# The output projection of a hybrid attention and pooling block by one level of Strassen's scheme

## Chip, core, metric

The kernel runs on one core of a Trainium2 chip. The metric is the device time of one execution in microseconds (us); lower is better. Engines: TensorE (PE: matmuls, and PEld: its weight loads), VectorE (DVE), ScalarE (ACT), GpSimd (POOL) and SyncE (SP), which here issues all DMAs. Each engine runs its own list of instructions in order and waits for the others by semaphores.

## The reference

One layer over 4096 tokens of width 1024, all in float32, cut to what matters:

```python
mod = c @ w_ada[l] + b_ada[l]
shift, scale, gate = jnp.split(mod, 3, axis=-1)
h = rms_norm(x, norm_g[l]) * (1.0 + scale[:, None, :]) + shift[:, None, :]
proj = h @ w_in[l]                       # q, k, v, u, z
...
a_out = chunk_attention(q, k, v, rel_bias[l])
p_out = multiscale_pool(u, w_pool[l], pool_scale[l])
y = jnp.concatenate([a_out, p_out], axis=-1) * jax.nn.silu(z)
x = x + gate[:, None, :] * (y @ w_out[l])
```

The change concerns the last line: y (4096 x 1024) times w_out (1024 x 1024), times a gate of each column, plus x.

## The kernel before

Tokens are cut into 32 blocks of 128, the contraction into 8 k-tiles of 128, the output columns into two halves of 512. For precision every float32 operand of a matmul is split into a high part `hi` (a cast to fp32r by ScalarE) and a rest `lo` (a subtraction of it, by GpSimd or VectorE): that is `split`, L95 to L97, which issues one instruction on each of the two engines. A product of two tiles then takes three matmuls: hi·hi, hi·lo and lo·hi.

The stages follow one another in the program, and a scheduler orders each engine's instructions by a simulated timeline. Stage A makes h, z, u and the pooled half of y. Stage B is the attention: 64 units (2 phases x 8 groups of tokens x 4 heads); `merge` weaves the parts of two units and the filler `work` of the unit together by position. Units 0 to 57 have the q, k, v projections as filler. Units 58 to 63 have the output projection of 12 blocks (`plan[58 + n // 2]`), of the first column half alone, since `y` of these blocks is complete by then. y lies transposed in DRAM (`yT_d`). Stage C, the last `with` of the program (L758 on), is the rest: 4 blocks of half 0, 16 blocks of both halves, 16 blocks of half 1. Its pools take memory that the attention's pools free at the end of unit 63; the gate's tiles (L760 to L762) are among them.

`out_items` (L412 to L443) is a block's work. For each column half it takes a PSUM tile `ps` (pool `pp`, two banks) and issues 8 x 3 matmuls (L428 to L430, each 128x512); while it runs, `load_h` (L102) loads and splits the next block's y (ScalarE and GpSimd). At the end VectorE multiplies `ps` by the gate (L435), x is added (L437: by GpSimd in the units, by VectorE in stage C), and the result is stored (L438). In all 32 x 2 x 24 = 1536 matmuls.

What comes at the swap of stages B and C: `load_wo(1, 2)` and `load_wo(1, 3)` for the last weights, `fin` of the last attention unit (L663, L664, L666 with `osum`), then `out_items` without other work.

## Time and profile before

| what | us |
|---|---|
| median of three runs (1988.44 to 1990.84) | 1988.89 |
| the profiled execution | 1987.33 |
| its span in the trace | 1985.0 |
| TensorE busy in it | 1932.2 (97%) |
| VectorE, ScalarE, GpSimd busy | 1139.5, 892.0, 852.1 |

The profiled execution is one execution, recorded by the hardware; between its span and its time lie 2.3 us that the trace does not cover. Matmuls overlap in the array, so a record's duration (392 ns) is longer than the distance of two matmuls. Line numbers are those of the kernel before; those of the changed kernel, where they are named, differ.

### The profile page before, as it was taken

The page shows a single profiled execution, that of the slowest core. Times are in us where ns is not written, and L with a number is a line of the kernel's source. Part 1 is how long each engine was busy: PE and PEld are TensorE (multiplying, and loading weights), DVE is VectorE, ACT ScalarE, POOL GpSimd, SP SyncE. Part 2 cuts the span into 40 slices and gives each one's busy share as a digit, 9 for nine tenths or more (in the row PEclk, how much of TensorE's full clock was granted, in tenths as well). Part 3 has the DMA queues.
Part 4 walks back from the last instruction along what each step waited for, and adds up shares of the span by engine and source line. Part 5 has one row for each costly group of instructions (what it writes and reads, how often), then busy time and mean ns, then how long its engine had stood idle before and what let it go on. Part 6 is the DMA issues. An engine that isn't in the chain of part 4 may idle for free.

```text
span 1985.0 us, 30104 instructions
## 1 busy us (share of the span) xinstructions
PE 1932.2 (97%) x10544; PEld 1659.5 (84%) x10544; DVE 1139.5 (57%) x2331; ACT 892.0 (45%) x1910; POOL 852.1 (43%) x1423
## 2 busy tenths in 40 slices
PE   6989999999999999999999999999999999999999
PEld 5778888888888898888889888888888788788887
DVE  7656554565644557666776666667666654433322
ACT  5422123221224556655676665656666754311121
POOL 6232332133046654454465556444364644322243
PEclk9999999999999999999999999999999999999999
DMA  9555344435432212221132222111121444544454
GB/s 329 195 175 161 93 146 138 149 108 154 142 122 65 68 51 59 56 62 47 55 91 86 62 78 75 50 53 54 53 65 44 139 138 134 159 142 147 147 181 164
DMA packets 172231, 220.15 MB, mean 111 GB/s; under 512 B 17456, under 2 KB 93744, under 8 KB 172080
## 3 DMA queue, kind: packets, MB, share of 16 engines
q1 hardware_dynamic: 172080, 218.23, 34.9%
q8 instruction: 83, 1.36, 0.3%
q14 instruction: 68, 0.56, 0.1%
HBM read 151.05 MB, written 58.74 MB: 106 GB/s over the span
## 4 chain that ended last, share of the span: by engine, by line
PE 88%; DVE 5%; DMA 3%; ACT 2%; issue 1%; POOL 1%; SPq 0%; DVEq 0%; POOLq 0%; ACTq 0%
PE ps L494 9%; PE ps L495 9%; PE ps L496 9%; PE ps L430 6%; PE ps L429 6%; PE ps L428 6%; PE ptps L622 6%; PE aps L297 4%; PE aps L298 4%; PE aps L296 4%; PE ps L297 4%; PE ps L298 4%; PE ps L296 4%; PE sps L582 3%; PE ops L641 3%; PE ops L640 3%
## 5 line engine op out<-in xcount | busy, mean ns | idle before, releaser
L97 POOL TENSOR_TENSOR bhl<-bhr,bhh 128x512 fp32r<-128x512 f32 x212 | 275.7, 1301 | 334.8 <-ACT bhh L96 322.4
L494 PE MATMUL ps<-w,bhh 128*128 128x512 f32 (+1 forms) x1024 | 354.3, 346 | 2.7 <-ACT qkr L507 2.5
L496 PE MATMUL ps<-w,bhl 128*128 128x512 f32 (+1 forms) x1024 | 351.5, 343 | 0.0
L495 PE MATMUL ps<-w,bhh 128*128 128x512 f32 (+1 forms) x1024 | 351.5, 343 | 0.0
L629 DVE TENSOR_TENSOR ptl<-ptps,pth 128x512 fp32r<-128x512 f32 x480 | 226.0, 486 | 167.8 <-ACT pth L628 163.8
L96 ACT CAST bhh<-bhr 128x512 fp32r<-128x512 f32 x224 | 138.7, 620 | 283.6 <-PE ps L429 177.7
L600 ACT ACTIVATE p<-p,mx 128x640 f32<-128x640 f32 (+4 forms) x256 | 204.6, 799 | 125.6 <-DVE mx L587 123.7
L628 ACT CAST pth<-ptps 128x512 fp32r<-128x512 f32 x480 | 193.8, 425 | 136.9 <-PE ptps L622 111.2
L587 DVE CUSTOM_DVE_ANT_0 p<-sps,nb 128x640 f32<-128x640 f32 (+4 forms) x256 | 198.8, 777 | 81.1 <-PE sps L583 78.1
L622 PE MATMUL ptps<-ident,p 128*128 128x128 f32 x1200 | 213.0, 274 | 0.3
L494 PEld LDWEIGHTS ps<-w,bhh 128*128 128x128 f32 x1024 | 193.5, 189 | 21.7 <-ACT qkr L507 3.6
L496 PEld LDWEIGHTS ps<-w,bhl 128*128 128x128 f32 x1024 | 193.6, 189 | 17.8
L495 PEld LDWEIGHTS ps<-w,bhh 128*128 128x128 f32 x1024 | 193.7, 189 | 17.5
L428 PE MATMUL ps<-w,bhh 128*128 128x512 f32 x512 | 200.8, 392 | 2.5 <-DVE qkr L435 2.1
L430 PE MATMUL ps<-w,bhl 128*128 128x512 f32 x512 | 200.7, 392 | 0.1
L429 PE MATMUL ps<-w,bhh 128*128 128x512 f32 x512 | 200.5, 392 | 0.0
L259 POOL TENSOR_TENSOR xt<-xt,rb 128x512 f32<-128x512 f32 x56 | 80.0, 1462 | 234.0 <-DMA rb<-rs_d 234.0
L640 PE MATMUL ops<-pth,v 128*128 128x512 f32 x480 | 162.7, 340 | 4.1 <-ACT pth L628 2.6
L582 PE MATMUL sps<-kr,qs 128*128 128x320 f32 (+2 forms) x480 | 156.3, 334 | 7.6 <-DVE mx L587 6.8
L622 PEld LDWEIGHTS ptps<-ident,p 128*128 128x128 f32 x1200 | 147.2, 140 | 19.7 <-DVE ql L547 0.7
L641 PE MATMUL ops<-ptl,v 128*128 128x512 f32 x480 | 155.2, 330 | 1.8 <-DVE ptl L629 1.3
L297 PE MATMUL aps<-hlo,w 128*128 128x512 f32 x392 | 154.2, 393 | 2.1 <-DVE hlo L97 2.1
(129 smaller groups left out, 3885.6 us busy)
## 6 DMA issues: line engine op xcount, KB each, us to landing
bhr<-hT_d SPq DMA_DIRECT2D x128, 256.0 KB, 2.8
bhr<-yT_d SPq DMA_DIRECT2D x96, 256.0 KB, 2.9
xt<-in_x_dram SPq DMA_DIRECT2D x32, 512.0 KB, 5.1
qkr<-in_x_dram SPq DMA_DIRECT2D x64, 256.0 KB, 3.4
out_dram<-qkr SPq DMA_DIRECT2D x64, 256.0 KB, 2.2
xt<-in_xT_dram SPq DMA_DIRECT2D x28, 512.0 KB, 6.2
hT_d<-xt SPq DMA_DIRECT2D x56, 256.0 KB, 2.3
w_s<-in_w_adaT_dram SPq DMA_DIRECT2D x16, 512.0 KB, 6.7
```

The costliest lines, as they stand in the source:

```text
L97: eng.tensor_tensor(lo, raw, hi.bitcast(F32), op=ALU.subtract)
L297: nc.tensor.matmul(ps, wh[:, cs], l_, start=False, stop=False)
L428: nc.tensor.matmul(ps, a_, wh, start=k == 0, stop=False)
L429: nc.tensor.matmul(ps, a_, wl, start=False, stop=False)
L430: nc.tensor.matmul(ps, l_, wh, start=False, stop=k == KT - 1)
L494: nc.tensor.matmul(ps, a_, wh, start=k == 0, stop=False)
L495: nc.tensor.matmul(ps, a_, wl, start=False, stop=False)
L496: nc.tensor.matmul(ps, l_, wh, start=False, stop=k == KT - 1)
L582: nc.tensor.matmul(o, QS[ph, sg, h][:, qc], ks[:, k0 : k0 + n], start=True, stop=False)
L622: nc.tensor.transpose(out=ps[:, i * P : (i + 1) * P], in_=Pt[ph, sg, h, i][:, w : w + P], identity=ident)
L629: nc.vector.tensor_tensor(l_[:, r], ps[:, r], a_[:, r].bitcast(F32), op=ALU.subtract)
L640: nc.tensor.matmul(o[:, r], v, a_[:, r], start=n == 0, stop=False, skip_group_check=True)
```

## The change

One level of Strassen's scheme (in Winograd's form, with fewer additions) for pairs of blocks p and p + 16: the two blocks of tokens, the two halves of the contraction and the two halves of the columns make a 2 x 2 problem, and seven products of quarters, of 12 matmuls each, take the place of eight. That is 84 matmuls a pair.

Two of the seven need no combination. They are the *osteps* (32 of them, each 4 k-tiles x 3 matmuls): `(0, p)` multiplies the first half of y of block p by the first quarter of the weights, and ScalarE copies the result (L470) to be stored in DRAM (`s1_d`); `(1, p)` adds the second half's product in the same PSUM bank and finishes the first column half of block p (L473 gate on VectorE, L474 x on GpSimd). Both use the `ps` tiles and `load`-ahead by two. 24 osteps are planned in the units 58 to 63, where 12 half blocks were, with as many matmuls (288); eight come behind.

Then stage C. `w_prep`, four times, loads four weight tiles of 128x512, makes three more from them (L811 and L813 on VectorE, L812 and L816 on GpSimd) and splits four (three on VectorE, one on GpSimd). The *steps* follow, five products per pair in the order (1,p), (3,p), (2,p+1), (4,p), (0,p), each 12 matmuls (L420 to L422). For a pair, `combine` makes four combinations of y's quarters on GpSimd (L841 to L844) and five splits (ScalarE, and VectorE L98); five additions out of PSUM (L864, L867, L868, L871, L874), three gate multiplies (L426) on VectorE and three additions of x on GpSimd (L427) end it. Each pair has 11 DMAs of 256 KB. The pools: `d_w` of 16 weight tiles (4 before), `dr` of 12 raw tiles, `dc` of 3, and two PSUM pools (`dy`, `dz`) of two banks each.

```diff
@@ -409,38 +410,72 @@
-    def out_items(key, b, ns, after=None):
...
+    def product(ps, a_, l_, W, start):
+        for k in range(4):
+            wh, wl = W[k]
+            nc.tensor.matmul(ps, a_[:, k, :], wh, start=start and k == 0, stop=False, skip_group_check=True)
+            nc.tensor.matmul(ps, a_[:, k, :], wl, start=False, stop=False, skip_group_check=True)
+            nc.tensor.matmul(ps, l_[:, k, :], wh, start=False, stop=k == 3, skip_group_check=True)
+
+    def finish(c, n, xr, b, eng):
+
+        nc.vector.tensor_tensor(c, c, gate[n], op=ALU.mult)
+        eng.tensor_tensor(c, c, xr, op=ALU.add)
+        nc.sync.dma_start(out[b * P : (b + 1) * P, n * 512 : (n + 1) * 512], c)
...
+    osteps = [(0, 0)]
+    for p in range(1, NPAIR):
+        osteps += [(0, p), (1, p - 1)]
+    osteps.append((1, NPAIR - 1))
...
+            raw = sh.tile([P, 4, P], F32, name="bhr", bufs=2)
+            sg, j = divmod(p, NB)
+            nc.sync.dma_start(raw, yT_d[sg][j, :, half * 4 : half * 4 + 4, :])
+            a_ = sh.tile([P, 4, P], F32R, name="bhh")
+            l_ = sh.tile([P, 4, P], F32R, name="bhl")
+            split(a_, l_, raw, nc.gpsimd)
...
+            wh, wl = WO[0, half * 4 + k]
+            nc.tensor.matmul(ps, a_[:, k, :], wh, start=half == 0 and k == 0, stop=False, skip_group_check=True)
+            nc.tensor.matmul(ps, a_[:, k, :], wl, start=False, stop=False, skip_group_check=True)
+            nc.tensor.matmul(ps, l_[:, k, :], wh, start=False, stop=k == 3, skip_group_check=True)
+            if k == 3:
+                OH.pop(i)
+                o_load(i + 2)
+                t = op.tile([P, 512], F32, name="qkr")
+                if half == 0:
+                    nc.scalar.copy(t, ps)
+                    nc.sync.dma_start(s1_d[p], t)
+                else:
+                    nc.vector.tensor_tensor(t, ps, gate[0], op=ALU.mult)
+                    nc.gpsimd.tensor_tensor(t, t, xr, op=ALU.add)
+                    nc.sync.dma_start(out[p * P : (p + 1) * P, 0:512], t)
...
-        for n, ko in enumerate(outs):
-            plan[58 + n // 2].append(ko)
+        for i in range(24):
+            plan[58 + i // 4].append(("o", i))
...
-        w3 = cd.enter_context(tc.tile_pool(name="d_w", bufs=4))
+        w3 = cd.enter_context(tc.tile_pool(name="d_w", bufs=16))
...
+        dr = cd.enter_context(tc.tile_pool(name="d_r", bufs=12))
+        dc = cd.enter_context(tc.tile_pool(name="d_c", bufs=3))
+        dy = cd.enter_context(tc.tile_pool(name="d_y", bufs=2, space=PSUM))
+        dz = cd.enter_context(tc.tile_pool(name="d_z", bufs=2, space=PSUM))
...
-        rest = [("r", b, [0]) for b in range(NOUT, NOUT + 4)]
-        rest += [("r", b, [0, 1]) for b in range(NOUT + 4, NBLK)] + [("s", b, [1]) for b in range(NOUT + 4)]
...
+        def w_prep(k):
+            r = {}
+            for i in range(2):
+                for n in range(2):
+                    r[i, n] = dr.tile([P, 512], F32, name="dr")
+                    nc.sync.dma_start(r[i, n], wo[:, 4 * i + k, n * 512 : n * 512 + 512])
+            nc.vector.tensor_tensor(r[0, 0], r[0, 1], r[0, 0], op=ALU.subtract)
+            nc.gpsimd.tensor_tensor(r[0, 1], r[1, 1], r[0, 1], op=ALU.subtract)
+            nc.vector.tensor_tensor(r[1, 1], r[1, 1], r[0, 0], op=ALU.subtract)
+            w_split(2, k, r[1, 1], nc.vector)
+            w_split(1, k, r[0, 0], nc.vector)
+            nc.gpsimd.tensor_tensor(r[1, 0], r[1, 0], r[1, 1], op=ALU.subtract)
+            w_split(3, k, r[0, 1], nc.vector)
+            w_split(4, k, r[1, 0], nc.gpsimd)
+        WT[0] = {k: WO[1, 4 + k] for k in range(4)}
...
+        steps = [(2, 0)]
+        for p in range(NPAIR):
+            steps += [(1, p), (3, p)] + ([(2, p + 1)] if p + 1 < NPAIR else []) + [(4, p), (0, p)]
...
+            g = nc.gpsimd
+            if t == 2:
+                s1 = RAW[p, 2, 0] = dr.tile([P, 4, P], F32, name="dr")
+                g.tensor_tensor(s1, RAW[p, 1, 0], RAW[p, 1, 1], op=ALU.add)
+                g.tensor_tensor(RAW[p, 1, 0], RAW[p, 0, 0], RAW[p, 1, 0], op=ALU.subtract)
+                g.tensor_tensor(RAW[p, 0, 0], s1, RAW[p, 0, 0], op=ALU.subtract)
+                g.tensor_tensor(RAW[p, 0, 1], RAW[p, 0, 1], RAW[p, 0, 0], op=ALU.subtract)
+            raw = {2: RAW[p, 0, 0], 1: RAW.get((p, 2, 0)), 3: RAW[p, 1, 0], 4: RAW[p, 1, 1], 0: RAW[p, 0, 1]}[t]
+            a_ = sh.tile([P, 4, P], F32R, name="bhh")
+            l_ = sh.tile([P, 4, P], F32R, name="bhl")
+            split(a_, l_, raw, nc.vector)
...
+            last = nc.vector if p == NPAIR - 1 else nc.gpsimd
+            a_, l_ = DH.pop((t, p))
+            product(ps, a_, l_, WT[t], t in (1, 2))
+            if t == 2:
+                U2[p] = dc.tile([P, 512], F32, name="u2")
+                nc.vector.tensor_tensor(U2[p], ps, SX[p], op=ALU.add)
+            elif t == 3:
+                c = op.tile([P, 512], F32, name="qkr")
+                nc.vector.tensor_tensor(c, ps, SX[p], op=ALU.add)
+                nc.vector.tensor_tensor(c, ZP[p], c, op=ALU.add)
+                finish(c, 1, xr, b2, nc.gpsimd)
+            elif t == 4:
+                nc.vector.tensor_tensor(SX[p], ps, SX[p], op=ALU.add)
+                finish(SX.pop(p), 0, xr, b2, nc.gpsimd)
+            elif t == 0:
+                nc.vector.tensor_tensor(U2[p], ps, U2[p], op=ALU.add)
+                finish(U2.pop(p), 1, xr, p, last)
+
+        for i in range(24, len(osteps)):
+            if i < 28:
+                w_prep(i - 24)
+            for f in o_items(i):
                 f()
-            if i in (1, 2):
-                load_wo(1, i + 1, w3, stage)
+            if i == 28:
+                fetch(0)
+        combine(*steps[0])
+        combine(*steps[1])
+        for i, (t, p) in enumerate(steps):
+            if t == 1 and p + 1 < NPAIR:
+                fetch(p + 1)
+            step(t, p)
+            if i + 2 < len(steps):
+                combine(*steps[i + 2])
```

**The swap, on GpSimd.** In the list before, this stands around the end of the last attention unit (`osum` is the attention's last result; `w` and `bhl` are lower parts of weights and of y):

```order
L97 TENSOR_TENSOR bhl<-bhr,bhh 128x512 x3
L606 COPY rlx<-rl 128x4x64
L666 TENSOR_TENSOR osum<-osum,gzb 128x512
L606 COPY rlx<-rl 128x4x64
L97 TENSOR_TENSOR w<-bhr,w 128x512 x2
L97 TENSOR_TENSOR bhl<-bhr,bhh 128x512 x2
L97 TENSOR_TENSOR w<-bhr,w 128x512 x2
L97 TENSOR_TENSOR bhl<-bhr,bhh 128x512 x2
L666 TENSOR_TENSOR osum<-osum,gzb 128x512
L97 TENSOR_TENSOR bhl<-bhr,bhh 128x512 x62
```

and this in the list after, from the same `osum` (the `dr` are weights or y's quarters, in combination; `qkr` are finished blocks):

```order
L701 TENSOR_TENSOR osum<-osum,gzb 128x512
L474 TENSOR_TENSOR qkr<-qkr 128x512
L812 TENSOR_TENSOR dr<-dr 128x512
L816 TENSOR_TENSOR dr<-dr 128x512
L812 TENSOR_TENSOR dr<-dr 128x512
L474 TENSOR_TENSOR qkr<-qkr 128x512
L98 TENSOR_TENSOR bhl<-bhr,bhh 128x512
L816 TENSOR_TENSOR dr<-dr 128x512
L98 TENSOR_TENSOR w<-dr,w 128x512
L812 TENSOR_TENSOR dr<-dr 128x512
L98 TENSOR_TENSOR bhl<-bhr,bhh 128x512
L98 TENSOR_TENSOR w<-dr,w 128x512
```

Behind `osum` came splits of y only, each with its own block; now the first 24 instructions behind it, up to the first L843, are a mixture of the weights' combinations and splits, osteps' splits and ends, and the first combinations of y.

**The swap, on TensorE.** L640 and L641 (L675 and L676 after) are the attention's last products, L622 (L657) its transposes; `ps` are the output projection. Before:

```order
L429 MATMUL ps<-w,bhh 128x512
L430 MATMUL ps<-w,bhl 128x512
L640 MATMUL ops<-pth,v 128x128
L641 MATMUL ops<-ptl,v 128x128
L428 MATMUL ps<-w,bhh 128x512
L429 MATMUL ps<-w,bhh 128x512
L640 MATMUL ops<-pth,v 128x256
L641 MATMUL ops<-ptl,v 128x256
L640 MATMUL ops<-pth,v 128x128
L641 MATMUL ops<-ptl,v 128x128
L430 MATMUL ps<-w,bhl 128x512
L428 MATMUL ps<-w,bhh 128x512
```

After, the same place:

```order
L675 MATMUL ops<-pth,v 128x384
L676 MATMUL ops<-ptl,v 128x384
L657 MATMUL ptps<-ident,p 128x128 x2
L675 MATMUL ops<-pth,v 128x128
L657 MATMUL ptps<-ident,p 128x128
L676 MATMUL ops<-ptl,v 128x128
L675 MATMUL ops<-pth,v 128x256
L676 MATMUL ops<-ptl,v 128x256
L675 MATMUL ops<-pth,v 128x128
L676 MATMUL ops<-ptl,v 128x128
L462 MATMUL ps<-w,bhh 128x512
L463 MATMUL ps<-w,bhh 128x512
```

The output matmuls stood among the attention's last ones; now they follow them. Behind row L462 there are 72 osteps' matmuls (six osteps), then the steps.

**The loop over pairs, on VectorE.** Before, the last stage of the projection had these two in turn to the end:

```order
L437 TENSOR_TENSOR qkr<-qkr 128x512
L435 TENSOR_TENSOR qkr<-ps,gate_19468 128x512
L437 TENSOR_TENSOR qkr<-qkr 128x512
L435 TENSOR_TENSOR qkr<-ps,gate_19468 128x512
L437 TENSOR_TENSOR qkr<-qkr 128x512
```

After, from one pair of blocks to the next (`s_`, `u_` and `qkr` hold sums, `zps` and `yps` are PSUM):

```order
L867 TENSOR_TENSOR qkr<-yps,s_19971 128x512
L98 TENSOR_TENSOR bhl<-dr,bhh 128x512
L868 TENSOR_TENSOR qkr<-zps,qkr 128x512
L426 TENSOR_TENSOR qkr<-qkr,gate_19534 128x512
L864 TENSOR_TENSOR u_20151<-yps,s_20090 128x512
L98 TENSOR_TENSOR bhl<-dr,bhh 128x512
L871 TENSOR_TENSOR s_19971<-yps,s_19971 128x512
L98 TENSOR_TENSOR bhl<-dr,bhh 128x512
L426 TENSOR_TENSOR s_19971<-s_19971,gate_19532 128x512
L874 TENSOR_TENSOR u_20032<-zps,u_20032 128x512
L98 TENSOR_TENSOR bhl<-dr,bhh 128x512
L426 TENSOR_TENSOR u_20032<-u_20032,gate_19534 128x512
```

With one more split that makes 13 instructions a pair, five of them out of PSUM. 

**The loop over pairs, on GpSimd.** Before there were only L97 splits of `bhl` (the last row of the first list). After:

```order
L427 TENSOR_TENSOR s_19754<-s_19754,qkr 128x512
L842 TENSOR_TENSOR dr<-dr 128x512
L427 TENSOR_TENSOR u_19838<-u_19838,qkr 128x512
L843 TENSOR_TENSOR dr<-dr 128x512
L844 TENSOR_TENSOR dr<-dr 128x512
L427 TENSOR_TENSOR qkr<-qkr 128x512
L841 TENSOR_TENSOR dr<-dr 128x512
L427 TENSOR_TENSOR s_19852<-s_19852,qkr 128x512
```

That is seven a pair, four combinations and three ends.

## Rows read from the trace of the kernel before

**Rows 1.** Page: busy time by engine; the chain that ended last, by engine.
```profile
PE 1932.2 (97%) x10544; PEld 1659.5 (84%) x10544; DVE 1139.5 (57%) x2331; ACT 892.0 (45%) x1910; POOL 852.1 (43%) x1423
...
PE 88%; DVE 5%; DMA 3%; ACT 2%; issue 1%; POOL 1%; SPq 0%; DVEq 0%; POOLq 0%; ACTq 0%
```

**Rows 2.** Windows: length, then PE, PEld, DVE, ACT, POOL busy, clock, DMA.
```profile
1740.00:1970.00 230.00, 230.00 (x1016) 190.48 (x1015) 75.81 (x85) 34.82 (x56) 74.41 (x57) 1.00 0.48 160
```

**Rows 3.** Groups by line: count; busy us, mean ns; idle before, releaser.
```profile
L428 PE MATMUL ps<-w,bhh 128*128 128x512 f32 x512 | 200.8, 392 | 2.5 <-DVE qkr L435 2.1 <-ACT bhh L96 0.4
```

**Rows 4.** Timeline of PE near the end: start, duration (us), engine, line.
```profile
1975.53 0.39 PE L428 MATMUL ps<-w,bhh 128*128 128x512 f32 x1
...
1979.61 0.39 PE L428 MATMUL ps<-w,bhh 128*128 128x512 f32 x1
```

**Rows 5.** Lines 435, 437: count, duration ns min/median/max, first and last start.
```profile
L437 DVE TENSOR_TENSOR qkr<-qkr x52: 675/693/1823, 1703.3 to 1981.2; 128x512 f32<-128x512 f32 x52
...
L437 POOL TENSOR_TENSOR qkr<-qkr x12: 1276/1292/1299, 1582.7 to 1676.7; 128x512 f32<-128x512 f32 x12
...
L435 DVE TENSOR_TENSOR qkr<-ps,gate x64: 673/691/692, 1581.2 to 1980.5; 128x512 f32<-128x512 f32 x64
```

**Rows 6.** Timeline of POOL, and of DVE beside it.
```profile
1653.54 1.30 POOL L437 TENSOR_TENSOR qkr<-qkr 128x512 f32<-128x512 f32 x1
1654.79 1.29 POOL L97 TENSOR_TENSOR bhl<-bhr,bhh 128x512 fp32r<-128x512 f32 x1
...
1806.93 1.29 POOL L97 TENSOR_TENSOR bhl<-bhr,bhh 128x512 fp32r<-128x512 f32 x1 [1.43 <-ACT bhh L96]
...
1807.14 1.63 DVE L437 TENSOR_TENSOR qkr<-qkr 128x512 f32<-128x512 f32 x1
```

**Rows 7.** Timeline at 44 us, where POOL and DVE are both saturated.
```profile
43.89 2.32 POOL L97 TENSOR_TENSOR hlo<-bhr,hhi 128x512 fp32r<-128x512 f32 x1
...
46.15 1.21 DVE L191 CUSTOM_DVE_ANT_0 w_s<-w_s,cb 128x1024 f32<-128x1024 f32 x1
...
46.18 2.34 POOL L97 TENSOR_TENSOR w<-bhh,w 128x512 fp32r<-128x512 f32 x1
```

**Rows 8.** Gate load, its eviction, PE's wait; the last attention matmul.
```profile
1698.50 0.80 SPq L762 DMA_DIRECT2D gate<-gate_d  x2
...
DMA to landing us min/median/max: 3.5/3.7/3.8
...
1702.14 1.29 DVE L435 TENSOR_TENSOR qkr<-ps,gate 128x512 f32<-128x512 f32 x2 [1.64 <-DMA gate<-gate_d]
...
1702.89 0.50 PE L428 MATMUL ps<-w,bhh 128*128 128x512 f32 x1 [2.10 <-DVE qkr L435]
...
1719.06 0.27 PE L641 MATMUL ops<-ptl,v 128*128 128x128 f32 x1
```

**Rows 9.** Groups by line from 1570 us: ScalarE's cast of a split.
```profile
L96 ACT CAST bhh<-bhr 128x512 fp32r<-128x512 f32 x96 | 59.6, 621 | 236.8 <-PE ps L429 177.7 <-DMA bhr<-yT_d 46.6 <-PE ps L430 6.9
```

**Rows 10.** Groups by line from 1570 us: what a block of probabilities passes.
```profile
L628 ACT CAST pth<-ptps 128x384 fp32r<-128x384 f32 (+3 forms) x63 | 24.8, 422 | 18.5 <-PE ptps L622 17.2 <-PE ops L640 0.9
...
L629 DVE TENSOR_TENSOR ptl<-ptps,pth 128x384 fp32r<-128x384 f32 (+2 forms) x64 | 29.9, 487 | 27.5 <-ACT pth L628 26.9
```

**Rows 11.** Windows at 115 us; the clock is the third column from the end.
```profile
115.00:121.00 6.00, 3.92 (x10) 3.12 (x10) 5.66 (x10) 1.66 (x3) 0.00 (x0) 0.50 1.03 297
121.00:122.00 1.00, 1.00 (x4) 0.77 (x4) 0.00 (x0) 0.00 (x0) 0.00 (x0) 0.62 0.99 264
122.00:124.00 2.00, 2.00 (x11) 1.62 (x10) 0.00 (x0) 0.48 (x1) 0.00 (x0) 1.00 1.03 401
```

**Rows 12.** Timeline at the end of the program.
```profile
1980.07 0.39 PE L430 MATMUL ps<-w,bhl 128*128 128x512 f32 x1
1980.49 0.69 DVE L435 TENSOR_TENSOR qkr<-ps,gate 128x512 f32<-128x512 f32 x1 [4.02 <-PE ps L430]
1981.22 0.69 DVE L437 TENSOR_TENSOR qkr<-qkr 128x512 f32<-128x512 f32 x1
```

106 lines of the change are left out of this document (55 added, 51 removed).

## The prediction

> **What bounds the kernel now.** I read the page first. TensorE is busy 97% of the span and holds 88% of the chain that ended last [rows 1], so the time is, nearly, TensorE's work plus its holes. Then the view by windows: in the 230 us of steady output projection at the end, TensorE has no hole and full clock, VectorE works 76 us, GpSimd 74 us, and the DMA engines carry 160 GB/s at a share of 0.48 [rows 2]. The groups by line put a matmul's record at 392 ns, but matmuls overlap; the whole projection waits 2.5 us, 2.1 of it once, for the gate [rows 3]. The pitch comes from the timeline: the same line, L428, starts at 1975.53 and at 1979.61, and 18 matmuls start in between [rows 4], so one costs 4.08/18 = 0.2267 us. In short: a matmul removed is worth 0.2267 us, if TensorE remains the engine that others are waiting for. Two stretches can make that untrue: the swap of stages, where weights must be combined, and the loop over pairs, where VectorE and GpSimd get far more work.
>
> **Removed matmuls.** 32 blocks x 2 halves x 24 = 1536 become 16 pairs x 84 = 1344: 192 x 0.2267 = **-43.5 us**.
>
> **What the new vector work costs: the two engines hinder each other.** GpSimd's add of two 128x512 tiles has records of 1290 ns and VectorE's multiply out of PSUM 691, never over 692; but VectorE's add of two SBUF tiles has a median of 693 and a maximum of 1823 [rows 5]. The timeline shows why: VectorE's add began at 1807.14, while GpSimd's subtract ran from 1806.93 to 1808.22, and ended 0.55 us after it [rows 6]. It is the reverse too: where both are saturated, GpSimd's subtracts start 2.29 us apart (43.89, 46.18), with VectorE's 128x1024 operation of 1.21 between [rows 7]. Alone, GpSimd starts every 1.25 us (1653.54, 1654.79) [rows 6]. So VectorE's 1024 columns pushed GpSimd by 1.04, and I take 0.52 for 512: the two behave as if they shared one way into SBUF, which a GpSimd operation holds for 1.25 and a VectorE operation with two SBUF inputs for 0.52, one after another. Operations that read PSUM go beside it.
> The Trainium skill (SBUF — State Buffer, "SBUF: two separate sides") says that the pair of ports shared by VectorE and GpSimd is an exclusive lock, held for the whole instruction. By that, taken as full records, the hold would be 1.29 + 0.69; the trace agrees that the loser stops, but its saturated rows, 2.29 for records of 1.28 and 1.21, show less than full records [rows 7].
>
> **The swap.** The tiles of the combined weights take memory that the last attention unit frees, so all of w_prep starts when that unit's last matmul is done (T0). Here is what must happen on GpSimd before the first combined product can begin, by the order: 24 operations of 128x512 behind L701, since the combined weights, the last osteps' splits and the first two pairs' combinations are woven into one another. VectorE has 19 two-SBUF operations and five L473 (PSUM) in that stretch. Lead-in: the first of the 24, L474, waits for L473, which waits for the gate's DMA. In before the gate was issued at 1698.50 and landed after 3.7, and both VectorE's eviction and TensorE waited for it [rows 8]. The last attention matmul there starts at 1719.06; in the new order the gate's load waits for the last such matmul. 3.7 + 0.69 = 4.4, say 4.5. Then 24 x 1.25 = 30.0 and 19 x 0.52 = 9.9, then a cast on ScalarE, 0.62 [rows 9], its signals and the split's start 0.2: **45.2 us** from T0. TensorE has 72 matmuls of osteps in it, 16.3 us, and nothing else that it may do: the first combined product, L420, is next in its queue. Idle **+28.9**. Bounds: no hindrance, 35.3 - 16.3 = 19.0; full records, 24 x 1.29 + 19 x 0.69 + 5.3 = 49.4, less 16.3 = 33.1. I take the middle value because its 0.52 is from the saturated rows, the nearest. The loads hide: 16 weight tiles and ten of the first two pairs are 6.8 MB; at 330 GB/s (an estimate: 160/0.48 [rows 2]) that is 21 us, ahead of GpSimd's pace.
>
> **Small terms.** (a) The last attention unit loses its fillers: in before output matmuls stood among its last matmuls, now they follow. A block of probabilities passes ScalarE's cast (0.43) and VectorE's subtract (0.49) [rows 10] before its products; TensorE's own work between is about 0.7 (two 512 products and up to four short transposes), so eight blocks uncover 0.2 each and the last one 0.9: **+2.5**; 0 if the queued work covers, 4 if half of every step shows. (b) The old holes go [rows 3]: **-2.5**. (c) In units 58 to 63 a product now ends every 12 matmuls in half of the cases with a copy on ScalarE behind its softmax work, with two banks: **+1** (0 to 2.6, a wait of 0.43, as long as a cast [rows 10], in each of six units). (d) Clock: in before, a long wait of TensorE at 114 us was followed by 6 us at a granted clock of 0.50 (the 1.2 GHz level) and one at 0.62, before 1.00 came back [rows 11]; TensorE was busy for 4.9 of those 7 us at about half pace, so some 11 matmuls cost 0.2 more each: **+2.2** (twice that if the idle comes in two pieces). (e) First and last pairs run without neighbours' work between product and eviction: three waits of an add, 0.7 each, less what overlaps: **+1.8** (0 to 4). (f) At the end three operations follow the last matmul (add, gate, add x), where two did, 0.69 each [rows 12]: **+0.7**.
>
> **The loop over pairs.** A pair's five products are 60 matmuls: 13.6 us. GpSimd has seven operations, VectorE 13, of which eight read two SBUF tiles (five splits, three gates): 7 x 1.25 + 8 x 0.52 = **12.9 us**, 0.7 under TensorE. VectorE's own time is 13 x 0.69 = 9.0, its blocked time in part behind GpSimd. Its 11 DMAs, 2.9 MB in 13.6 us, are 212 GB/s, above the 160 here but well under 330. Splits are three tiles ahead and combinations a pair ahead, so a late operation need not stop TensorE. I take **0**; the bound on the other side is full records, 7 x 1.29 + 8 x 0.69 = 14.55, or 0.95 x 16 = +15.2. What hides it is thin: 5% of the period.
>
> **Sum.** -43.5 + 28.9 + 2.5 - 2.5 + 1 + 2.2 + 1.8 + 0.7 = -8.9. The profiled execution took 1987.3 (span 1985.0 and 2.3 around it), so 1978.4 by its account; the median of the runs is 1.6 higher, 1988.9, and against that I predict **1980.0 us**.
>
> **Rivals.** *The swap is cheaper.* If operations on GpSimd lie in VectorE's PSUM gaps and the two seldom meet, or L474 is early, the idle falls to 19 and below: 1970; with no re-warm and no lost attention cover, 1964. For it: the median of VectorE's adds is that of an operation nobody hinders [rows 5]. Against it: there GpSimd is busy a third of the time [rows 2], here without pause. 0.17.
> *The pair loop is bound by the shared way into SBUF* (ends slower). The mechanism: GpSimd and VectorE in the loop over pairs, each in its own fixed order; whenever GpSimd waits for a gate multiply that stands on VectorE behind a split, or VectorE for a product, the way stands empty, and only 0.7 per period may. Price: with full holds 14.55 a pair, 1980 + 15.2 = **1995**. It decides from a period of 14.15 (8.9 us gone over 16 pairs is 0.55). For it: 95% use of a way that two engines with their own waits share is hard to keep up; against it: the combinations run ahead and fill. 0.25. *Halfway*, a period of 13.9 to 14.4: 1985 to 1993, 0.18.
> By the rule of the Trainium skill's page SBUF — State Buffer ("SBUF: two separate sides"), the lock lasts the whole instruction; that would be this rival's 14.55, and the saturated rows speak for less [rows 7].
> *That the change doesn't do what it says*: the steps are 80 x 12 = 960 matmuls (L420 to L422) and the osteps 384 (L462 to L464), 1344 in all, and the order has them so. No chance.
>
> **How the numbers follow.** Forecast, 1974 to 1985: 0.40; swap cheaper, 1958 to 1974: 0.17; halfway 0.18; loop-bound, over 1993: 0.25. The range that leaves out the lower half of the cheap swap and the upper part of the loop-bound case is 1966 to 1998. What a measurement can tell from no change is 0.2%, 4 us: faster below 1984.9 0.57, same to 1992.9 0.18, slower 0.25.
>
> **What would show it.** Right: TensorE empty for some 29 us between the last L676 and the first L420 (osteps' L462 to L464 aside), GpSimd busy nearly all of it with starts 1.77 us apart where it alternates with VectorE; granted clock at 0.50 behind that; then a steady pitch of 0.2267 with a pair every 13.6 us and no hole. Wrong: holes in front of L420 in the loop, released by VectorE's split or GpSimd's combination (the period then tells which rival), or idle at the swap under 20 us; or waits of TensorE for ScalarE's copy L470 in units 58 to 63 of more than 3 us.

## The result: 1978.0 us, 10.9 us faster

The changed kernel takes 1977.99 us (median of four runs, 1977.33 to 1978.80), the kernel before, beside it, 1988.85 us (1988.44 to 1990.84). The ratio is 0.9944, with a 95% interval of 0.9931 to 0.9958: faster by 0.56%, clearly more than the 0.2% that can be told from no change. Predicted were 1980.0 us, in a range of 1966 to 1998.

The profiled execution after took 1978.80 us with a span of 1977.0, against 1987.33 and 1985.0. The spans differ by 8.0 us, the medians by 10.9: the profiled execution before lies 1.5 us under its median, the one after is the slowest of its four. The account below is made from the spans.

The page, busy time and the chain that ended last, answering [rows 1]:

```profile
PE 1895.7 (96%) x10352; PEld 1625.4 (82%) x10352; DVE 1268.1 (64%) x2460; ACT 916.7 (46%) x1954; POOL 951.0 (48%) x1482
...
PE 81%; DVE 8%; DMA 5%; ACT 3%; issue 2%; POOL 1%; SPq 0%; DVEq 0%; POOLq 0%; ACTq 0%
```

TensorE has 192 matmuls fewer (10544 and 10352) and is busy 36.5 us less, but the chain runs through it for 81% of the span and not 88%: VectorE, DMA and ScalarE have taken six of the seven points. Where, the windows tell (columns as in [rows 2]: length, then busy time of PE, PEld, DVE, ACT, POOL, granted clock, DMA share and GB/s). First the swap, from the last attention matmul to the first combined product, and two pieces of it; then the first 9.5 us of products; then the steady loop, answering [rows 2]:

```profile
1703.40:1750.50 47.10, 21.36 (x73) 15.71 (x73) 31.30 (x27) 13.52 (x25) 38.36 (x26) 0.76 0.74 250
1728.40:1731.50 3.10, 3.10 (x9) 2.33 (x8) 3.10 (x2) 2.21 (x4) 3.10 (x3) 0.50 0.93 285
1740.00:1750.50 10.50, 0.05 (x1) 0.05 (x1) 1.98 (x3) 1.34 (x3) 10.50 (x9) 0.58 0.47 159
1750.50:1760.00 9.50, 9.50 (x32) 7.61 (x33) 7.01 (x6) 2.19 (x4) 8.79 (x7) 0.74 0.23 78
1780.00:1960.00 180.00, 180.00 (x796) 149.05 (x795) 156.64 (x174) 41.58 (x67) 130.90 (x88) 1.00 0.62 201
```

In the loop TensorE has no hole in 180 us: the pairs run at TensorE's pitch, with VectorE busy 87% and GpSimd 73%. In the swap TensorE stands still for more than half of the time, in its last 10 us altogether. The timeline of TensorE shows the holes, in brackets how long it had idled and what ended it:

```profile
1703.08 0.28 PE L676 MATMUL ops<-ptl,v 128*128 128x128 f32 x1
...
1710.29 0.80 PE L462 MATMUL ps<-w,bhh 128*128 128x512 f32 x1 [6.94 <-DVE qkr L473]
...
1727.27 0.50 PE L462 MATMUL ps<-w,bhh 128*128 128x512 f32 x1 [3.85 <-DVE qkr L473]
...
1750.45 0.80 PE L420 MATMUL yps<-w,bhh 128*128 128x512 f32 x1 [11.63 <-ACT bhh L97]
```

The last attention matmul ends at 1703.4, the first product (L420) starts at 1750.45: 47.1 us, in which 72 matmuls of osteps lie (16.3 us at the pitch of [rows 4]). So 30.8 us are lost there. TensorE stands still in 25.8 of them (6.94, 1.33, 0.41, 3.85, 1.62 and 11.63); the rest is mostly osteps at a lower clock, behind the holes of 6.94 and 3.85 (granted clock 0.50, the 1.2 GHz level, in the row from 1728.40). GpSimd's list in the same place, and one row of VectorE:

```profile
1710.32 1.27 POOL L474 TENSOR_TENSOR qkr<-qkr 128x512 f32<-128x512 f32 x1 [4.23 <-DVE qkr L473]
...
1716.98 1.74 POOL L474 TENSOR_TENSOR qkr<-qkr 128x512 f32<-128x512 f32 x1
1718.69 1.74 POOL L98 TENSOR_TENSOR bhl<-bhr,bhh 128x512 fp32r<-128x512 f32 x1
...
1729.90 6.85 DVE L98 TENSOR_TENSOR w<-dr,w 128x512 fp32r<-128x512 f32 x4
...
1743.62 1.26 POOL L474 TENSOR_TENSOR qkr<-qkr 128x512 f32<-128x512 f32 x1
1744.84 1.26 POOL L842 TENSOR_TENSOR dr<-dr 128x512 f32<-128x512 f32 x1
...
1748.49 1.25 POOL L843 TENSOR_TENSOR dr<-dr 128x512 f32<-128x512 f32 x1
```

The first of the 24 operations starts at 1710.32 and the last ends at 1749.74. Fifteen of the 24 are lengthened by an operation of VectorE on two SBUF tiles: behind them the next one starts after 1.63 to 1.73 us, 1.68 in the mean (1.71 between 1716.98 and 1718.69), and four of VectorE's splits take 6.85 us; when VectorE has nothing (from 1742 on it waits for ScalarE's cast), GpSimd starts every 1.22 us. The gate's load, answering [rows 8], was slower than before. Three loads of weights of 256 KB are issued in the 1.4 us ahead of it, from 1702.22 on. In the kernel with the pools in another order (below), where no load stands close ahead of it and eight follow, it landed after 4.0; so the loads ahead are the likely cause, though no run tests them alone:

```profile
L791 SPq DMA_DIRECT2D gate<-gate_d x2: 376/404/431, 1703.6 to 1704.0; - x2
...
DMA to landing us min/median/max: 5.9/6.2/6.5
```

And the end of the program, answering [rows 12]:

```profile
1971.49 0.39 PE L422 MATMUL zps<-w,bhl 128*128 128x512 f32 x1
...
1971.91 0.69 DVE L874 TENSOR_TENSOR u<-zps,u 128x512 f32<-128x512 f32 x1 [1.30 <-PE zps L422]
...
1972.64 0.69 DVE L426 TENSOR_TENSOR u<-u,gate 128x512 f32<-128x512 f32 x1
1973.36 0.69 DVE L427 TENSOR_TENSOR u<-u,qkr 128x512 f32<-128x512 f32 x1
```

**The account**, each term beside what the trace gives for it:

| term | predicted | measured | from |
|---|---|---|---|
| 192 matmuls less | -43.5 | -43.5 | 1536 and 1344 at 0.2267 |
| swap: last attention matmul to first product | 45.2 | 47.1 | 1703.36 to 1750.45 |
| of it uncovered (72 matmuls off) | +28.9 | +30.8 | 47.1 - 16.3 |
| attention's end without fillers, evictions in units 58 to 63 | +3.5 | +1.0 | first output matmul to last attention matmul: 147.1 before, 129.3 after, with 74 output matmuls less (-16.8) and the gate's hole gone (-2.1) |
| old holes | -2.5 | -2.1 | [rows 3] |
| slow clock, first and last pair | +4.0 | +3.6 | first to last product: 221.0 for 959 pitches (217.4) |
| the loop's other holes | 0 | 0 | windows above |
| end | +0.7 | +0.6 | last matmul to end: 4.9 before, 5.5 after |
| stages ahead of the change | 0 | +1.9 | first output matmul at 1572.2 before, 1574.1 after |
| sum | -8.9 | -7.7 | spans: -8.0 |

The 1.9 us ahead of unit 58 fall in lines that the change doesn't touch; it is a difference of executions: in the traces of the changed kernel and of the twelve below this first output matmul starts anywhere from 1572.2 to 1574.6. With it gone the account would give -9.6, still 1.3 short of the medians' -10.9.

### The profile page after: what moved, and what is told of

It reads as the page before. It is cut to its first block, busy times and chain, and to the rows that moved or that the text cites. A ratio compares the mean times of both kernels' runs of the same rounds, so it can differ in the third digit from the quotient of the medians.

```text
span 1977.0 us, 30086 instructions
## 1 busy us (share of the span) xinstructions
PE 1895.7 (96%) x10352; PEld 1625.4 (82%) x10352; DVE 1268.1 (64%) x2460; ACT 916.7 (46%) x1954; POOL 951.0 (48%) x1482
## 3 DMA queue, kind: packets, MB, share of 16 engines
q8 instruction: 81, 1.33, 0.3%
## 4 chain that ended last, share of the span: by engine, by line
PE 81%; DVE 8%; DMA 5%; ACT 3%; issue 2%; POOL 1%; SPq 0%; DVEq 0%; POOLq 0%; ACTq 0%
PE ps L529 9%; PE ps L530 9%; PE ps L531 9%; PE ptps L657 6%; PE aps L298 3%; PE ps L298 3%; PE aps L299 3%; PE ps L299 3%; PE aps L297 3%; PE ps L297 3%; PE ops L676 3%; PE sps L617 3%; PE ops L675 3%; PE sps L618 3%; PE yps L420 2%; PE yps L421 2%
## 5 line engine op out<-in xcount | busy, mean ns | idle before, releaser
L98 POOL TENSOR_TENSOR bhl<-bhr,bhh 128x512 fp32r<-128x512 f32 x148 | 192.1, 1299 | 156.8 <-ACT bhh L97 144.4
L622 DVE CUSTOM_DVE_ANT_0 p<-sps,nb 128x640 f32<-128x640 f32 (+4 forms) x256 | 199.0, 777 | 84.0 <-PE sps L618 80.7
L657 PE MATMUL ptps<-ident,p 128*128 128x128 f32 x1200 | 213.2, 274 | 0.3
L675 PE MATMUL ops<-pth,v 128*128 128x512 f32 x480 | 162.9, 340 | 5.3 <-ACT pth L663 2.8
L657 PEld LDWEIGHTS ptps<-ident,p 128*128 128x128 f32 x1200 | 147.1, 140 | 19.6 <-DVE ql L582 0.7
L676 PE MATMUL ops<-ptl,v 128*128 128x512 f32 x480 | 155.6, 331 | 1.9 <-DVE ptl L664 1.2
L297 PE MATMUL ps<-hhi,w 128*128 128x512 f32 x376 | 146.9, 394 | 7.9 <-DVE gz L306 7.9
L297 PE MATMUL aps<-hhi,w 128*128 128x512 f32 x392 | 152.5, 392 | 0.2 <-ACT w L97 0.2
L299 PE MATMUL aps<-hhi,w 128*128 128x512 f32 x392 | 152.4, 392 | 0.0
L298 PE MATMUL ps<-hlo,w 128*128 128x512 f32 x376 | 147.2, 391 | 2.5 <-POOL hlo L98 2.5
```

The costliest lines, as they stand in the source:

```text
L297: nc.tensor.matmul(ps, wh[:, cs], a_, start=k == 0, stop=False)
L298: nc.tensor.matmul(ps, wh[:, cs], l_, start=False, stop=False)
L299: nc.tensor.matmul(ps, wl[:, cs], a_, start=False, stop=k == KT - 1)
L657: nc.tensor.transpose(out=ps[:, i * P : (i + 1) * P], in_=Pt[ph, sg, h, i][:, w : w + P], identity=ident)
L675: nc.tensor.matmul(o[:, r], v, a_[:, r], start=n == 0, stop=False, skip_group_check=True)
L676: nc.tensor.matmul(o[:, r], v, l_[:, r], start=False, stop=last, skip_group_check=True)
```

## The experiments

Line names below are those of the changed kernel. In the profiles of kernels with added or removed lines they are shifted, by up to eight, and in the first kernel by 25 behind `w_prep` (its L842 is L867).

### What the swap costs, and whom

**Without the combined weights.** Left out is `w_prep`; the five products use one quarter of the weights.

```diff
+        WT = {t: {k: WO[1, 4 + k] for k in range(4)} for t in range(5)}
...
-            if i < 28:
-                w_prep(i - 24)
```

> Left out: the weights' loads, combinations and splits of w_prep; all five products of a pair use the fourth quarter of the weights instead. Every matmul, every combination of y and every ending stays. If the swap's idle time of TensorE is the price of w_prep on GpSimd and VectorE (my account), nearly all of the 30.8 us that TensorE idles between the last attention matmul and the first combined product, and the 2 us of slow clock behind it, go: 3 to 8 us of idle remain for the first y tiles, so 1948 to 1955 us. If the stage change itself costs it (gate's load, y's loads, memory that is freed), the time stays above 1968.

1946.8 us (1945.0 to 1947.4), 31.2 less than with the weights. All that TensorE waited for from 1570 us on (waits: what, for whom; total us, times, longest):

```profile
PE ps L462 <- DVE qkr L473: 1.6, 1, 1.6
PE ops L675 <- DVE osum L699: 1.0, 1, 1.0
PE yps L420 <- DVE qkr L842: 0.9, 1, 0.9
PE sps L617 <- DVE mx L622: 0.9, 2, 0.6
```

And the issue of the gate's load:

```profile
1694.92 0.80 SPq L791 DMA_DIRECT2D gate<-gate_d  x2
```

So the swap's idle time goes when the preparation goes: 1.6 us in front of an ostep are all that is left of it, less than I had left. But the kernel leaves out more than work. Without combined weights nothing is put into the 64 KB pool, and the stage's other tiles move up, it seems, to memory that is free earlier: the gate's load is issued at 1694.92, 18.9 us ahead of the end of the last attention matmul (1713.77), where the changed kernel issues it 0.25 us behind that end. The 31.2 us are therefore the price of the weights with the memory that they take; about 1947 is what would be left if both were hidden.

**The preparation on VectorE alone.** Twelve operations move from GpSimd to VectorE.

```diff
-            nc.gpsimd.tensor_tensor(r[0, 1], r[1, 1], r[0, 1], op=ALU.subtract)
+            nc.vector.tensor_tensor(r[0, 1], r[1, 1], r[0, 1], op=ALU.subtract)
...
-            nc.gpsimd.tensor_tensor(r[1, 0], r[1, 0], r[1, 1], op=ALU.subtract)
+            nc.vector.tensor_tensor(r[1, 0], r[1, 0], r[1, 1], op=ALU.subtract)
...
-            w_split(4, k, r[1, 0], nc.gpsimd)
+            w_split(4, k, r[1, 0], nc.vector)
```

> The twelve GpSimd operations of w_prep (two combinations and one split for each of four k-tiles) go to VectorE; the same loads, the same data. Shared way (a GpSimd operation holds 1.23, a VectorE one with two SBUF inputs 0.45 by the spacing of the trace after): GpSimd has about 15 operations in front of the first product, VectorE 33: 15 x 1.23 + 33 x 0.45 + 5.3 = 38.6 us instead of 47, so about 8 us faster, 1968 to 1972 us. If GpSimd's queue alone sets it: 15 x 1.23 + 5.3 = 24, 20 us or more faster, below 1960. If the loads of 6.8 MB set it: no change, 1976 to 1979.

1971.39 us (1969.90 to 1974.86; ratio to before 0.9913, 0.9898 to 0.9928): 6.6 us faster than the change, at the edge of what the shared way expects. The last attention matmul starts at 1702.7, the first product now at 1744.1: 41 us and not 47. GpSimd's queue alone (20 us faster) and the loads alone (nothing) are both out. Twelve times the difference of the holds (1.22 and 0.46) would be 9.1 us; less came, since VectorE's queue is now the longer one. From 1711.15 to 1741.03 it has 35 operations, 0.60 us apart where nothing hinders them, and GpSimd is left waiting (windows of the swap; GpSimd, the fifth busy time, works 19.4 of 41 us):

```profile
1703.00:1744.00 41.00, 21.57 (x72) 15.96 (x72) 32.30 (x38) 13.52 (x25) 19.39 (x13) 0.78 0.80 276
```


**The gate kept.** Its tiles come from a pool that lives to the end; the second load is gone.

```diff
+    gp = ctx.enter_context(tc.tile_pool(name="b_gate", bufs=1))
...
-        for n in range(2):
-            gate[n] = gp.tile([P, 512], F32, name=f"gate{n}")
-            nc.sync.dma_start(gate[n], gate_d[:, n * 512 : (n + 1) * 512].broadcast_to([P, 512]))
```

> The gate's tiles live to the end of the program instead of being loaded again behind the last attention unit. Nothing else changes in the text, but the scheduler now draws all osteps in front of the last attention matmul, so nothing is left to cover the swap. If the swap's length is the queue on GpSimd and VectorE: 16 GpSimd operations and 19 of VectorE stay, 3.3 + 16 x 1.23 + 19 x 0.45 + 0.8 = 32 us without cover, where now 30.8 us are uncovered: 1976 to 1982. If the late gate (first eviction 6.2 us behind the last attention matmul) is what costs: 7 us faster, 1971.

1979.36 us (1978.14 to 1980.57), no gain. In front of the first product there is one hole now (waits of TensorE; then GpSimd's first operation on a weight):

```profile
PE yps L421 <- ACT bhh L97: 35.2, 1, 35.2
...
1721.42 1.26 POOL L807 TENSOR_TENSOR dr<-dr 128x512 f32<-128x512 f32 x1 [2.21 <-DMA dr<-in_w_out_dram]
```

The late gate had held the osteps back, and so had made them cover. Without it they run earlier, and the same work of GpSimd and VectorE lies bare: 35.2 us (32 expected). A wait that looked like a loss of 7 us was none. Nor does GpSimd start at once without it: its first operation on a weight comes 4.9 us behind the last attention matmul (end 1716.53), and waits for the weights' own load.

**TensorE kept busy in the hole.** Forty matmuls that nobody reads, before the first product.

```diff
+        warm = dq.tile([P, SG], F32, name="warm")
+        for n in range(40):
+            nc.tensor.matmul(warm, tail[:, 3, :], WO[0, 0][0], start=True, stop=True, skip_group_check=True)
```

> Forty matmuls of 128x512, into a PSUM tile that nobody reads, run between the last ostep and the first combined product, in TensorE's hole of 11.6 us (40 x 0.2267 = 9.1). If the slow clock behind the hole is worth 2.2 us and comes from the hole, the products start at full clock and the kernel is 2 us faster (1975 to 1977), with a granted clock near 1.0 in the 10 us after the first product. If the clock does not follow the hole, or is hidden: no change, and the clock stays at 0.74 there.

1976.98 us (1976.28 to 1977.46): 1.0 us faster, half of what was expected, and less than two kernels can be told apart by; the trace has to decide. The hole shrank from 11.6 to 2.8 us, yet the clock still fell behind it (timeline, then the windows; clock third from the end):

```profile
1748.97 0.50 PE L420 MATMUL yps<-w,bhh 128*128 128x512 f32 x1 [2.76 <-ACT bhh L97]
...
1751.13 0.63 PE L421 MATMUL yps<-w,bhh 128*128 128x512 f32 x1
1751.56 0.63 PE L422 MATMUL yps<-w,bhl 128*128 128x512 f32 x1
...
1751.00:1753.50 2.50, 2.50 (x7) 1.92 (x7) 2.43 (x2) 0.00 (x0) 1.88 (x2) 0.50 0.24 69
1753.50:1756.00 2.50, 2.50 (x12) 2.06 (x12) 1.72 (x2) 0.62 (x1) 2.49 (x2) 0.99 0.37 141
1750.00:1760.00 10.00, 10.00 (x38) 8.07 (x38) 7.30 (x7) 1.74 (x3) 9.21 (x7) 0.83 0.29 90
```

Starts are 0.43 us apart from 1750.7 to 1753.3 (granted clock 0.50, the 1.2 GHz level), and 0.23 behind that (0.99, the 2.4 GHz level). In the changed kernel the same ten microseconds had 32 matmuls in 9.5 us where the pitch makes 42, a loss of 2.2 us, as predicted; here the clock of 0.83 still takes 38 where 44 would fit. So the slow clock is real and follows the hole, and here it came behind one of only 2.8 us.

### What the loop over pairs can carry

**One and two more operations of GpSimd per pair**, from pair 2 on, into a tile that nobody reads.

```diff
+                if p >= 2:
+                    for _ in range(1):
+                        g.tensor_tensor(spare, RAW[p, 0, 1], RAW[p, 0, 0], op=ALU.subtract)
```

> One more GpSimd subtraction of 128x512 per pair, from pair 2 on, into a tile that nobody reads. Loop under TensorE with slack: by the prediction's prices 8 x 1.25 + 8 x 0.52 = 14.2 us a pair against TensorE's 13.6, so 14 x 0.6 = +8 us; by the spacing in the swap of the trace after (1.23 and 0.45) 13.4, so still hidden: within 2 us of the changed kernel. If the loop were already bound there: +17 us.

> Two more GpSimd subtractions per pair from pair 2 on. By the prediction's prices 15.4 us a pair: +25 us; by those of the swap in the trace after (1.23, 0.45) 14.7: +14 to +16 us; GpSimd alone (9 x 1.25 = 11.3) would hide it: no change.

With one: 1976.77 us (1975.46 to 1978.55), no cost that can be told. With two: 1987.14 us (1985.94 to 1989.81), +9.1 us. The windows of the later pairs, first with one, then with two, and the wait that appears with two (up to 1958 us), with the first and the seventh of its rows, which come once a pair:

```profile
1860.00:1950.00 90.00, 90.00 (x399) 74.53 (x398) 86.28 (x87) 20.61 (x33) 87.12 (x53) 1.00 0.61 202
```

```profile
1860.00:1950.00 90.00, 83.45 (x363) 67.30 (x362) 82.37 (x80) 18.28 (x31) 88.59 (x55) 1.00 0.59 193
...
PE yps L420 <- DVE qkr L871: 6.5, 6, 1.1
...
1871.91 0.47 PE L420 MATMUL yps<-w,bhh 128*128 128x512 f32 x1 [1.14 <-DVE qkr L871]
...
1961.62 0.47 PE L420 MATMUL yps<-w,bhh 128*128 128x512 f32 x1 [1.09 <-DVE qkr L871]
```

With one more, TensorE still has no hole, while GpSimd is at 87.1 of 90 us. With two, TensorE waits once a pair, and six pairs take 89.71 us (1871.91 to 1961.62), 14.95 each. This gives the hold of a VectorE operation: 9 x 1.22 + 8 x h = 14.95, h = 0.50 at most, since GpSimd has no other waits of note there (busy 88.6 of 90 us). The swap's spacing gives 0.46 (1.68 - 1.22). My 0.52 and 1.25 were a few per cent too dear: the changed loop needs at most 7 x 1.22 + 8 x 0.50 = 12.5 us of TensorE's 13.6, and with one more operation 13.4 to 13.8. The rival of full records (14.55 a pair) is refuted by the first kernel, since the loop has room for another operation. That two more cost 9 and not 14 to 16 is the lead of a pair that the combinations have: TensorE has no such hole before 1871.91, and eight of them behind it, 8.6 us in all.

### Better orders

**Another order** of the swap: gate kept; weights combined and split on VectorE, the first product's first; the last six osteps load y into `dr` (20 tiles instead of 12), to stay behind as cover.

```diff
-        dr = cd.enter_context(tc.tile_pool(name="d_r", bufs=12))
+        dr = cd.enter_context(tc.tile_pool(name="d_r", bufs=20))
...
+            raw = dr.tile([P, 4, P], F32, name="dr") if i >= 26 else sh.tile([P, 4, P], F32, name="bhr", bufs=2)
...
+        def w_first(k):
+            for i, n in ((0, 1), (0, 0), (1, 1)):
+                r = rw[k, i, n] = dr.tile([P, 512], F32, name="dr")
+                nc.sync.dma_start(r, wo[:, 4 * i + k, n * 512 : n * 512 + 512])
...
+            w_split(2, k, rw[k, 1, 1], v)
...
+                if steps[i + 2] in ((3, 0), (4, 0)):
+                    w_rest(steps[i + 2][0])
```

> The same products, with the swap put in another order: the gate's tiles live to the end; the last six osteps take their y tiles from memory that is freed by the attention, so they stay behind it as cover; weights are combined and split on VectorE for one product after the other (those of the first product first), so that the first product waits for about 17 VectorE operations and not for all 36 and 24 of GpSimd. By the shared way: cover of 16.3 us starts some 5 us behind the last attention matmul, the first product can start at about 22 us, and later gaps come to 3 to 6 us: idle 9 to 14 instead of 30.8, so 1957 to 1963 us. If loads or the sum of the work bound the swap whatever the order: 32 + 16 operations still in front of the fourth product, 1970 or more.

1984.01 us (1982.01 to 1985.00): a miss, 6 us slower than the change. The timeline of the DMA issues, and TensorE's first matmul behind the attention:

```profile
1706.83 0.37 SPq L335 DMA_DIRECT2D yT_d<-osum  x1
1709.26 1.28 SPq L805 DMA_DIRECT2D dr<-in_w_out_dram  x3
...
1717.37 0.80 PE L463 MATMUL ps<-w,bhh 128*128 128x512 f32 x1 [13.30 <-ACT bhh L97]
```

No weight is loaded before 1709.26, 2.4 us behind the issue of the store of the attention's last result (L335), where the changed kernel issued its first at 1702.2. The reading: the larger `dr` reaches into the memory that this result lies in, and its tiles, the last osteps' y among them, wait until the store has landed. The tile sizes in the program agree with it, if pools lie one behind the other as they are opened: the attention's work pool, which holds `osum`, begins 94 KB behind its first pool (90 without the gate's tiles); the changed kernel's `dr` ends at 92, this one's at 104. So the cover came 13.3 us late, and the order had no fair trial.

**The pools in another order**, nothing else: raw tiles, gate and sums ahead of the 64 KB of weights.

```diff
-        w3 = cd.enter_context(tc.tile_pool(name="d_w", bufs=16))
-        gp = cd.enter_context(tc.tile_pool(name="d_g", bufs=1))
         dr = cd.enter_context(tc.tile_pool(name="d_r", bufs=12))
+        gp = cd.enter_context(tc.tile_pool(name="d_g", bufs=1))
         dc = cd.enter_context(tc.tile_pool(name="d_c", bufs=3))
+        w3 = cd.enter_context(tc.tile_pool(name="d_w", bufs=16))
```

> The changed kernel with one difference: of the last stage's pools, the raw tiles, the gate and the sums are opened ahead of the 64 KB of combined weights, so that they lie on the memory of the attention's biases and keys, which is free some 20 us before the last attention matmul, and the weights lie behind. No instruction is added or left out. If the swap's length is the queue behind freed memory: part of the weights' combinations now runs under the last attention unit, 12 GpSimd operations and 14 of VectorE stay behind it (12 x 1.23 + 14 x 0.45 + 2 = 23 us instead of 47), while 48 osteps' matmuls (10.9 us) move ahead of it: 13 us faster, 1963 to 1968. If the memory does not come free earlier, or the work only moves: 1976 to 1979.

1972.15 us (1971.89 to 1972.85): 5.8 us faster, not 13. The raw tiles are indeed loaded from 1695.1 on and combined under the attention, but the hole before the first product is 22.5 us, and ScalarE's first cast of a weight ends its wait on that store:

```profile
PE yps L420 <- ACT bhh L97: 22.5, 1, 22.5
...
1722.64 5.29 ACT L97 CAST w<-dr 128x512 fp32r<-128x512 f32 x10 [3.75 <-DMA yT_d<-osum]
```

Now the weights' tiles lie on the last result's memory (by the same count they end at 104 KB).

**Raw tiles early, in the other order**, without and with the last four osteps held behind the attention (`late`, two tiles of freed memory).

```diff
+        dr = cd.enter_context(tc.tile_pool(name="d_r", bufs=17))
         w3 = cd.enter_context(tc.tile_pool(name="d_w", bufs=16))
+        late = cd.enter_context(tc.tile_pool(name="d_l", bufs=2))
...
+        fetch(0)
```

> As the kernel of the other order (weights for one product after the other, on VectorE, the gate kept), but with the raw tiles opened first, on memory that is freed early, and 17 of them: the loads and combinations of twelve raw weight tiles and of the first pair's y run under the last attention unit. Behind its last matmul stay sixteen splits (VectorE, 0.69 each, and ScalarE) and four combinations. No cover is left, since all osteps run ahead. First product some 6 us behind the last attention matmul, three more gaps of 2 to 3 us until the fourth product's weights are there: 10 to 14 us of idle against 30.8 (and 1 to 2 us less of slow clock): 1957 to 1963. If the other order was slow for another reason than late memory: 1970 or more.

> As the kernel with the early raw tiles, but the last four osteps take their y tiles from memory that is free only behind the attention, so that 48 to 84 osteps' matmuls (11 to 19 us) stay as cover of the splits. If cover is what the swap then lacks: idle 3 to 7 us, 1950 to 1956. If the wait of the late osteps' own loads (about 5 us) is in front of everything: the same as without, within 3 us.

1974.44 us (1972.84 to 1976.32) and 1975.05 us (1973.81 to 1978.02): neither gains what was hoped, and the second comes out as said for the case that the late loads stand in front. Where TensorE waited in the first of them:

```profile
PE yps L421 <- ACT w L97: 12.9, 1, 12.9
PE yps L421 <- ACT bhh L97: 5.6, 1, 5.6
PE ops L677 <- DVE ptl L665: 5.0, 2, 4.7
...
1716.61 1.60 DVE L807 TENSOR_TENSOR dr<-dr 128x512 f32<-128x512 f32 x1
...
1735.37 6.34 ACT L97 CAST w<-dr 128x512 fp32r<-128x512 f32 x12 [9.93 <-DMA yT_d<-osum]
```

12.9 us go to the weights' casts, which begin at 1735.37, again behind the store of the last result (the weights' pool ends at 98 KB here, with the work pool from 90 on). That store had become late itself: the product in front of it stood on GpSimd behind the new combinations, and its issue on SyncE behind a load that waited for a free tile. And 5.0 us go to the attention: VectorE, in order, had three combinations of weights, lengthened by GpSimd's to 1.15 to 1.75 us each, and a gate multiply in front of the attention's subtract, from 1716.61 to 1721.5. Work that was moved ahead delayed what it should hide under. With the four held osteps the hole lies before them (12.0 us, for their loads, which are issued at 1721.80, again behind that store).

**Cover from PSUM.** `dr` at 12 tiles again, the first pair's y in a pool of its own, weights in the other order; and the osteps of the last pairs take the PSUM banks that the attention's transposes give back, so that with everything loaded they can't run before.

```diff
-                XP[p] = (pp.tile([P, SG], F32, name="ps"), load_xr(p, 0))
+                XP[p] = (dz.tile([P, SG], F32, name="zps") if p >= 13 else pp.tile([P, SG], F32, name="ps"), load_xr(p, 0))
...
+        d2 = cd.enter_context(tc.tile_pool(name="d_r2", bufs=5))
```

> As the other order (weights combined and split on VectorE for one product after the other, the gate kept), with two differences. Twelve raw tiles of weights stay one pool, so that this pool does not touch the memory of the attention's last result, and the first pair's y tiles have a pool of their own; and the last six osteps of the first half use PSUM banks that the attention's transposes give back, so that 96 osteps' matmuls (21.8 us) stand behind the last attention matmul with nothing left to wait for. Queue theory: some 28 VectorE and 10 GpSimd operations before the first product, 28 x 0.65 + 10 x 0.8 = 26 us behind the last attention matmul, of which 21.8 are covered; 4 us more of gaps before the fourth product's weights: idle 6 to 12 instead of 30.8, 1954 to 1962. If the order is not what failed there but late loads in any order: 1970 or more.

1962.25 us (1960.95 to 1963.81; ratio to before 0.986, 0.9844 to 0.9877): 15.7 us faster than the change. TensorE's holes over a microsecond in the swap, and the first weights' load:

```profile
1702.79 4.18 SPq L806 DMA_DIRECT2D dr<-in_w_out_dram  x9
...
1717.56 0.50 PE L463 MATMUL zps<-w,bhh 128*128 128x512 f32 x1 [1.71 <-DVE qkr L474]
1724.63 0.50 PE L463 MATMUL zps<-w,bhh 128*128 128x512 f32 x1 [4.05 <-ACT bhh L97]
1726.40 0.80 PE L465 MATMUL zps<-w,bhl 128*128 128x512 f32 x1 [1.03 <-POOL bhl L98]
1732.09 0.50 PE L421 MATMUL yps<-w,bhh 128*128 128x512 f32 x1 [1.81 <-ACT bhh L97]
1735.36 0.80 PE L423 MATMUL yps<-w,bhl 128*128 128x512 f32 x1 [1.53 <-DVE bhl L98]
```

Loads start at 1702.8, before the attention has ended, with the same instructions that started at 1709.3 in the first try. The 25.8 us of standing still have become 10.1, which is the 15.7 gained, and no hole is longer than 4.05. The first osteps on the new banks run from 1703.78 on, right behind the attention. The other order with its loads in time and the cover came together here; no run has the one without the other.

**The first pair's y early**, in the 10 KB that the attention never used:

```diff
+    d2 = ctx.enter_context(tc.tile_pool(name="d_r2", bufs=5))
...
-        d2 = cd.enter_context(tc.tile_pool(name="d_r2", bufs=5))
```

> As the kernel with the cover, but the first pair's five y tiles lie in memory that the attention never used (10 KB), so that their loads and four GpSimd combinations happen during the last units. Behind the last attention matmul GpSimd has then nine operations and not fourteen in front of the first products, and the 1.3 MB of loads is gone from the full queue there. Shared way: four or five GpSimd holds of 1.23 and the y loads less on the path of the first product: 4 to 6 us faster than with the cover alone, 1955 to 1959. If VectorE's 28 operations alone set the first product: no gain, 1960 to 1963.

**1958.99 us** (1957.69 to 1961.99; ratio to before 0.9851, 0.9833 to 0.9869), the fastest of all: 30 us under the kernel before and 19 under the change, at the far end of the expectation. The 3.3 us under the kernel with the cover alone are less than their intervals can tell. The first product starts at 1724.6, 21 us behind the last attention matmul. Twelve of the 31 us that the kernel without combined weights gained are still out.

## Why the prediction was right

- **The matmuls**: 43.5 us, by count and pitch; the pitch holds in the new loop (no hole in 180 us). Right.
- **The swap**: the step that carried the prediction, +28.9, measured +30.8. Its parts: the 24 operations of GpSimd, with VectorE's 19 between them, took 1710.32 to 1749.74, 39.4 us, predicted 30.0 + 9.9; the remainder behind them 0.7, predicted 0.8. Mis-sized was the lead-in: 7.0 us and not 4.5, for the gate's load landed in 6.2 us and not in the 3.7 of [rows 8], with three loads of 256 KB issued right ahead of it. I had taken the price of a load from a quiet place and used it in a full one. That the gate is not the cause of the loss, the kernel with the gate kept shows; some lead-in stays there, 4.9 us, by the weights' own loads. And TensorE was not empty for all of the 30.8: 25.8 are holes, and the rest is the osteps' slow clock, which the sign I gave (29 us empty) had left out.
- **The hindrance**: right in kind. The single holds were both a little dear (1.25 and 0.52, measured 1.22 and 0.46), and only 15 of the 24 operations, not 19, are lengthened by one; but GpSimd also waited 3.1 us for VectorE's results, which I had at nothing, and 24 x 1.22 + 15 x 0.46 + 3.1 = 39.3 comes near my 39.9. That these three errors cancel is luck. The Trainium skill (SBUF — State Buffer, "SBUF: two separate sides") says that the loser blocks for the whole instruction; the runs agree that it blocks, and that operations from PSUM don't take part (676 to 692 ns in the loop), but what an operation takes from the other engine is less than its record of 0.69 and 1.29 us. By full records the loop would have needed 14.55 us a pair, and the kernel with one more operation shows that it does not.
- **The loop**: 0, right, and with more room than I gave it (1.1 us a pair, not 0.7). The rival that ended slower, at 0.25, decides from a period of 14.15; the period is 13.6, and the kernel with two more operations, at 14.95, shows what it would have looked like.
- **Attention's end and evictions**: +3.5 predicted, +1.0 measured, the worst term by share. ScalarE's and VectorE's steps lay deeper beside TensorE's than eight uncovered blocks of 0.2: TensorE's longest wait there is 1.0, for the half-result L699.
- **Clock**: 2.2 us predicted, 2.2 lost in the first ten microseconds of products. Not predicted: the clock fell twice before, behind the holes of 6.9 and 3.85 us in front of osteps, and that did not lengthen the swap, since GpSimd's queue set its end.
- **The cheap swap** (0.17) did not come: GpSimd and VectorE meet at 15 of the 24 operations.
- **The sum**: the swap was 1.9 us too small and the attention's end with the evictions 2.5 too big. That they nearly cancel, and the total came within 2 us, is luck too.

Open: how the 31 us of the kernel without combined weights divide into their work and the late start that their memory brings is not measured; the pools in another order moved only part of it (5.8 us). That a pool waits as a whole for the memory of the last result is read from four kernels' loads and casts and from tile sizes, not from a test of its own.

## What to carry to other kernels

When arithmetic is saved on the bound engine, price the stretch where the new operands are made by the queue of the engines that make them, operation by operation, with their hold on each other; it is the first product that pays. Something must stand ready on the bound engine for that long, and what holds it ready may be a resource (the PSUM banks here) more than an order in the program. Before work is moved ahead, look what its memory still belongs to: a tile on memory whose last use is a store waits for the store to land, and in-order queues hand that wait to everyone behind.
